# A hybrid attention layer on one core: a stated order on ScalarE and VectorE for the first rotated tiles

## The chip, the cores and the metric

The kernel runs as one program on 1 core of a Trainium2 chip. The metric is the device time of one execution in microseconds (us). Before the change three runs took 1109.55, 1108.88 and 1105.74 us; their median is 1108.88. A core has TensorE (PE: matmuls, and PEld: loading their weights), VectorE (DVE), ScalarE (ACT), GpSimd (POOL) and SyncE (SP, which here only issues transfers). Each works through its own queue of instructions in order and waits for the others through semaphores.

## What is computed

One encoder layer over 1024 tokens of width 1024, in float32. The input is normed and projected once; the columns of the projection feed two attentions, whose normed outputs go through one output projection, and then a gated MLP with a short convolution follows. What the change touches is the start of the first attention (8 query heads in 2 groups, each with one key and one value head, a window of 128 tokens to each side, and rotary embedding on a quarter of the dimensions):

```python
hn = rmsnorm(h, norm_mix[l])
proj = jnp.einsum('bsd,de->bse', hn, w_in[l])
qa, ka, va, qb, kb, vb = jnp.split(proj, splits, axis=-1)
qa = partial_rope(qa.reshape(B, S, A_HEADS, HEAD_DIM), cos, sin)
ka = partial_rope(ka.reshape(B, S, A_KV_HEADS, HEAD_DIM), cos, sin)
va = va.reshape(B, S, A_KV_HEADS, HEAD_DIM)
o_a = window_gqa_sink(qa, ka, va, sink[l])
o_b = neighbourhood_attention(...)
...
def partial_rope(t, cos, sin):
    half = ROT_DIM // 2
    x1 = t[..., :half]
    x2 = t[..., half:ROT_DIM]
    return jnp.concatenate([x1 * cos - x2 * sin, x2 * cos + x1 * sin, t[..., ROT_DIM:]], axis=-1)
```

## The kernel before

**Tiles.** Everything is kept with features in partitions and tokens along the free axis. The input projection is made in 18 tiles `m` of 128 features. For the first head group, m = 0 holds the key head (partitions 0 to 63) and the value head (64 to 127), and m = 1 and 2 hold two query heads each; m = 3, 4, 5 are the same for the second group. From m = 6 on come the tiles of the second attention.

**Precision.** A float32 factor is split into a high part, which ScalarE makes with a copy, and a low part, which VectorE makes by subtracting the high part from the source. `halve_w` does so for weights (L126 high, L127 low), in halves of four blocks of 128 rows: `load_w` and `Project.load` take blocks 0 to 3, `Project.load_rest` takes 4 to 7. A product is then three matmuls a block (L134 to L136: high by high, high by low, low by high); a tile of 128 features by 1024 tokens takes two halves `h` of 512 tokens, each of 8 blocks, so 24 matmuls. The high and the low weights have three buffers each, the raw weights two.

**From a projected tile to the scores.** A half tile stands in a PSUM bank until `evacuate` (L189, VectorE) multiplies it by the norm's reciprocal and writes it to the tile `t`. Projections use two banks by turns ("pj"); the first three tiles use others as well. Then, for m = 0 to 5, `post` runs:

- `split_v` (m = 0 and 3 only): TensorE transposes the value half (L269), ScalarE copies it (L273), VectorE makes the low part (L274).
- `rotate`: transfers fold the rows to be rotated out into a compact tile `f` (L205: one on ScalarE's queue, one on SyncE's); VectorE multiplies, multiplies and adds (L207 twice, L208, L209); SyncE sends the rows back into `t` (L211 twice). There are three sets of scratch for it: two in the tile `f`, one in `turns`.
- the stacks: the tile, split in high and low parts, laid out in 128 partitions as the scores need it. For the first group no transfers are used: `split_first_k` makes `ka` and `kb` with two ScalarE copies (L235, L238) and two VectorE subtractions (L236, L237), `split_first` makes two `q` tiles with two ScalarE copies (L228) and two VectorE operations (L229).

A score tile (L309) is two matmuls of such stacks into one of two "s" banks. `softmax` frees the bank: VectorE adds the mask and takes the row extremum (L331), ScalarE takes the exponential with a sum (L335), VectorE inverts the sums of a pair of tiles (L337), GpSimd scales (L339). TensorE then transposes the tiles (L371), and so on.

**Order.** TensorE's order is that of the source (`manual_schedule`). On the other engines a scheduler picks by priority among what is ready by its own estimate; `tc.high_priority` lifts a block. The projections are a generator, `rest()`, whose steps (one block of three matmuls each) are woven between the attention's steps by `fill`. The first three tiles are projected before it starts, m = 2 with weights of its own (`raw3`, `whi3`, `wlo3`). `FILL0 = 22` steps run before the first scores: the 16 of m = 3, and 6 of m = 4. The stacks of m = 2 are made by `settle` within `rest()`, those of m = 0 and 1 ahead of it. m = 4's second weights are traced at step 11 (`REST`) of m = 3. The tile `t` of m = 0 to 3 is cut from one pool of three buffers (`tmp`), so m = 3's `t` needs a buffer that an earlier tile has left.

Of the kernel before, what the change touches and what calls it, by code (L numbers as in the profile page):

```python
# [53 lines left out]
def hybrid_layer(tc, xT, w_in, w_out, w_gate, w_up, w_down, small, sink, rpb, consts, rope, out):  # L54
    nc = tc.nc
    with ExitStack() as ctx:
# [13 lines left out]
        def big(name, tag, dt=F32):  # L70
            return lpool.tile([128, S], dt, name=name, tag=tag, bufs=slots[tag])
# [42 lines left out]
            nc.tensor.matmul(warm_ps[:, 0:128], ones, ones, start=True, stop=True)  # L114


        def fetch_w(src):

            raw = wpool.tile([128, 4, 128], F32, name="raw", tag="raw", bufs=2)
            nc.sync.dma_start(raw, src)  # L120
            return raw

        def halve_w(raw):

            hi, lo = (wpool.tile([128, 4, 128], F32R, name=n, tag=n) for n in ("whi", "wlo"))
            nc.scalar.activation(hi, raw, AF.Copy)  # L126
            nc.vector.tensor_tensor(lo, raw, f32(hi[:, :, :]), op=ALU.subtract)  # L127
            return [(hi[:, j, :], lo[:, j, :]) for j in range(4)]

        def load_w(src):  # L130
# [55 lines left out]

        def evacuate(t, ps, h, grid):
            if not grid:
                nc.vector.tensor_tensor(t[:, tsl(h)], ps, rstd1[:, tsl(h)], op=ALU.mult)  # L189
            else:  # L190
                v = lambda ap: ap.rearrange("p (r b c) -> p r b c", b=NB, c=8)
                o = t[:, :].rearrange("p (b r c) -> p r b c", r=ROWS, c=8)[:, 8 * h:8 * h + 8]
                nc.vector.tensor_tensor(o, v(ps[:, :]), v(rstd1[:, tsl(h)]), op=ALU.mult)

        folded = []

        def rotate(t, n):

            m = slice(0, n)
            f, u = folded[0]  # L200
            folded.append(folded.pop(0))
            rows = lambda s: t[4 * s:n:8].rearrange("a (c w) -> a c w", w=128)
            fold = lambda s: f[m, s]
            for s in range(2):
                (nc.scalar, nc.sync)[s].dma_start(fold(s), rows(s))  # L205
            for s in range(2):
                nc.vector.tensor_tensor(u[m, s], f[m, 1 - s], rs[m, s], op=ALU.mult)  # L207
            nc.vector.tensor_tensor(f[m], f[m], rc[m], op=ALU.mult)  # L208
            nc.vector.tensor_tensor(f[m], f[m], u[m], op=ALU.add)  # L209
            for s in range(2):  # L210
                nc.sync.dma_start(rows(s), fold(s))  # L211

        def split_pair(t):

# [9 lines left out]
        def split_first(t):  # L224

            a, b = big("q", "op", F32R), big("q", "op", F32R)
            for x, hi, lo in ((a, slice(0, 64), slice(64, 128)), (b, slice(64, 128), slice(0, 64))):
                nc.scalar.activation(x[hi], t[hi], AF.Copy, scale=-HD ** -0.5)  # L228
                nc.vector.scalar_tensor_tensor(x[lo], t[hi], -HD ** -0.5, f32(x[hi, :]), op0=ALU.mult, op1=ALU.subtract)  # L229
            return [a, b]  # L230

        def split_first_k(t):
            a, b = big("ka", "op", F32R), big("kb", "op", F32R)
            up, down = slice(0, 64), slice(64, 128)
            nc.scalar.activation(a[up], t[up], AF.Copy)  # L235
            nc.vector.tensor_tensor(b[up], t[up], f32(a[up, :]), op=ALU.subtract)  # L236
            nc.vector.tensor_tensor(a[down], t[up], f32(a[up, :]), op=ALU.subtract)  # L237
            nc.scalar.activation(b[down], t[up], AF.Copy)  # L238
            return a, b
# [13 lines left out]
        def split_k(t, e):  # L253

            a, b = big("ka", "op", F32R), big("kb", "op", F32R)
            o = 64 - e
            nc.scalar.activation(a[e:e + 64], t[e:e + 64], AF.Copy)
            nc.sync.dma_start(f32(b[o:o + 64, :]), f32(a[e:e + 64, :]))
            nc.vector.tensor_tensor(b[e:e + 64], t[e:e + 64], f32(a[e:e + 64, :]), op=ALU.subtract)
            nc.sync.dma_start(f32(a[o:o + 64, :]), f32(b[e:e + 64, :]))  # L260
            return a, b

        def split_v(t, halves):

            v = [big("v", "op", F32R) for _ in halves]
            for g in range(2):
                ps = bank("vt", "pt")
                for c in range(4):
                    nc.tensor.transpose(ps[:, c * 128:(c + 1) * 128], t[:, (4 * g + c) * 128:(4 * g + c + 1) * 128], ident)  # L269
                for i, e in enumerate(halves):  # L270
                    src = ps[:, :].rearrange("p (c w) -> p c w", w=128)[:, :, e * 64:e * 64 + 64]
                    dst = v[i][:, :].rearrange("p (c w) -> p c w", w=128)[:, 4 * g:4 * g + 4]
                    nc.scalar.activation(dst[:, :, 0:64], src, AF.Copy)  # L273
                    nc.vector.tensor_tensor(dst[:, :, 64:128], src, f32(dst[:, :, 0:64]), op=ALU.subtract)  # L274
            return [x[:, :].rearrange("p (c w) -> p c w", w=128) for x in v]

        qa, ka, va, qb, kb, vb = {}, {}, {}, {}, {}, {}
        mix = [None] * 8

        def post(m, t):  # L280

            if m < 6:
                g, i = divmod(m, 3)
                if i == 0:
                    va[g] = split_v(t, (1,))[0]
                    rotate(t, 64)
                    ka[g] = split_k(t, 0) if g else split_first_k(t)
                else:
                    rotate(t, 128)
                    qa[g, i - 1] = split_pair(t) if g else split_first(t)  # L290
            else:
                hp, i = divmod(m - 6, 3)
                if i == 0:
                    vb[2 * hp], vb[2 * hp + 1] = split_v(t, (0, 1))
                else:
                    h = 2 * hp + i - 1
                    qb[h], kb[h] = split_qk(t)
# [183 lines left out]
        class Project:  # L481
# [10 lines left out]
            def run(self):  # L492
                self.t = tmp("t")
                if self.m < 17:
                    for h in range(2):
                        ps = bank("pj", "pj")
                        yield from product(ps, self.w, xg, h)
                        with tc.high_priority(offset=500):
                            evacuate(self.t, ps, h, self.grid)
                else:  # L500

                    ps = [bank("pj", "pj") for _ in range(2)]
                    for k in range(KT):
                        for h in range(2):
                            block(ps[h], self.w[k], xg[k], h, k == 0, k == KT - 1)
                            yield
                        if k % 2:
                            mg[k // 2] = split(mix[k // 2], "mg", "xg")
                    for h in range(2):
                        evacuate(self.t, ps[h], h, self.grid)  # L510
# [84 lines left out]
        nc.scalar.activation(hi, raw, AF.Copy)  # L595
        nc.vector.tensor_tensor(lo, raw, f32(hi[:, :]), op=ALU.subtract)
        third.w = [(hi[:, 128 * k:128 * k + 128], lo[:, 128 * k:128 * k + 128]) for k in range(KT)]
        third.t = tmp("t")
        ps3 = [bank("s", "s") for _ in range(2)]
        for _ in product(ps3[0], third.w, xg, 0):  # L600
            pass
# [14 lines left out]
        for _ in rest3:  # L616
            pass
        for p in first:
            with tc.high_priority(offset=400):
                p.post()  # L620
        for h in range(2):
            evacuate(third.t, ps3[h], h, False)

        live = {"op": 0}
        needs = lambda m: 2 if m < 6 and m % 3 else 2 if m >= 6 and m % 3 == 0 else 3
        waiting = [third]

        def settle(age):

            while waiting and (len(waiting) > 1 or age >= (LATE if waiting[0].m == 3 else LAG)):  # L630
                m = waiting[0].m
                if live["op"] + needs(m) > slots["op"]:
                    break
                live["op"] += needs(m)
                with tc.high_priority(offset=400 if m == 2 else 0):
                    waiting.pop(0).post()

        aux = {}
# [1 line left out]
        def rest():  # L640
            for i, job in enumerate(jobs[1:]):
                if i + 2 < len(jobs):
                    jobs[i + 2].load()
                for n, _ in enumerate(job.run()):
                    yield True
                    if n == REST and i + 2 < len(jobs):
                        jobs[i + 2].load_rest()
                    settle(n)
                    if (i, n) in aux:
                        aux[i, n]()  # L650
                if isinstance(job, Project):
                    waiting.append(job)
                while len(waiting) > 2:
                    settle(0)
                    if len(waiting) > 2:
                        yield False
# [18 lines left out]
        for i in range(4):  # L675
            aux[13, 3 * i + 3] = normed_a(i)
        filler = rest()
        live["op"] = sum(needs(m) for m in (0, 1))

        def fill(n):  # L680
            while n > 0 and next(filler, False):
# [736 lines left out]
```

## Time and profile before

| | |
|---|---|
| runs, us | 1109.55, 1108.88, 1105.74 |
| median, us | 1108.88 |
| profiled execution: its own time, us | 1108.75 |
| its span, from first to last instruction, us | 1106.7 |
| mean granted clock of TensorE | 0.995 |
| TensorE busy | 98% of the span |
| VectorE / ScalarE / GpSimd busy | 77% / 50% / 10% |

The durations below come from the one profiled execution. Its own time is 2.05 us longer than its span. In a row of the timeline stand the start in us from the span's beginning, the duration, the engine, the line of the kernel, the operation, the tile written and those read, the sizes, how many such rows were merged, and in brackets how long the engine had been idle and which instruction it had waited for. "ACTq" and "SPq" are the engines' queues that issue transfers. Matmuls are pipelined, so the start of the next one, not the shown duration, is their pace.

### The profile page before, as it was taken

What the parts mean: (1) busy time and instruction counts of PE and PEld (TensorE: products, weight loads), DVE (VectorE), ACT (ScalarE), POOL (GpSimd) and SP (SyncE); (2) the same over time, 40 slices, a digit from 0 to 9 for tenths busy, and PEclk for the clock granted to TensorE, in tenths of its full rate; (3) what the DMA queues carried; (4) which work ended last, traced back from release to release, by engine and by line L of the source; (5) the groups of instructions that cost most, each with busy time, mean ns of one, the idle gap of its engine ahead of it and who ended that gap; (6) DMA issues with size and microseconds to landing.
All of it is one profiled execution on the core that took longest, in us unless ns stands there. A gap on an engine that the chain in (4) does not pass through costs nothing.

```text
span 1106.7 us, 15054 instructions
## 1 busy us (share of the span) xinstructions
PE 1082.4 (98%) x5190; PEld 903.6 (82%) x5190; DVE 857.7 (77%) x1565; ACT 551.6 (50%) x1041; POOL 108.7 (10%) x188
## 2 busy tenths in 40 slices
PE   9989999999999999999999999999999999999997
PEld 7868888888888888787788888888888878888887
DVE  7478888667688687899988877877887868886844
ACT  7257766656666544454444334342434644544531
POOL 2213333222232100000000000000000000000001
PEclk9999999999999999999999999999999999999999
DMA  7213122232225237304433222323322889874734
GB/s 270 71 51 79 49 66 65 70 86 67 77 64 156 68 106 264 106 11 145 167 121 127 105 105 96 113 97 116 104 86 105 272 287 300 267 224 159 270 95 153
DMA packets 68364, 144.94 MB, mean 131 GB/s; under 512 B 8128, under 2 KB 18880, under 8 KB 68288
## 3 DMA queue, kind: packets, MB, share of 16 engines
q1 hardware_dynamic: 57632, 118.16, 34.4%
q10 hardware_dynamic: 10656, 25.82, 6.2%
q8 instruction: 40, 0.66, 0.2%
q14 instruction: 36, 0.29, 0.1%
HBM read 103.58 MB, written 28.57 MB: 119 GB/s over the span
## 4 chain that ended last, share of the span: by engine, by line
PE 84%; DVE 9%; DMA 3%; ACT 2%; issue 2%; ACTq 0%; POOL 0%; SPq 0%; DVEq 0%; POOLq 0%
PE dn L826 6%; PE pj L134 6%; PE dn L828 6%; PE dn L827 6%; PE pj L135 6%; PE pj L136 6%; PE z L828 5%; PE z L826 5%; PE z L827 5%; PE s L309 3%; PE x L826 3%; PE x L827 3%; PE x L828 3%; PE y L828 3%; PE y L827 3%; PE y L826 3%
## 5 line engine op out<-in xcount | busy, mean ns | idle before, releaser
L826 PE MATMUL dn<-xd,whi 128*128 128x512 f32 (+1 forms) x330 | 124.9, 378 | 2.8 <-ACT c L1254 2.8
L828 PE MATMUL dn<-xd,wlo 128*128 128x512 f32 (+1 forms) x330 | 124.2, 376 | 0.0
L827 PE MATMUL dn<-xd,whi 128*128 128x512 f32 (+1 forms) x330 | 124.2, 376 | 0.0
L815 ACT ACTIVATE whi<-ws 128x512 fp32r<-128x512 f32 (+1 forms) x100 | 60.1, 623 | 124.1 <-DVE ws L932 82.5
L134 PE MATMUL pj<-xgh,whi 128*128 128x512 f32 x248 | 104.6, 422 | 3.1 <-DVE t L189 3.1
L828 PE MATMUL z<-hg,wlo 128*128 128x512 f32 x264 | 103.1, 390 | 0.6 <-DVE wlo L816 0.6
L826 PE MATMUL z<-hg,whi 128*128 128x512 f32 x264 | 103.0, 390 | 0.2 <-DVE gs L982 0.2
L827 PE MATMUL z<-hg,whi 128*128 128x512 f32 x264 | 102.7, 389 | 0.0
L335 ACT ACTIVATE p<-p,nm 128x385 f32<-128x385 f32 (+3 forms) x128 | 74.9, 586 | 46.9 <-DVE nm L331 46.2
L136 PE MATMUL pj<-xgh,wlo 128*128 128x512 f32 x248 | 98.3, 396 | 0.0
L135 PE MATMUL pj<-xgl,whi 128*128 128x512 f32 x248 | 98.0, 395 | 0.0
L339 POOL TENSOR_SCALAR p<-p,sm 128x384 f32<-128x384 f32 (+1 forms) x128 | 73.4, 586 | 222.0 <-DVE sm L337 207.4
L816 DVE TENSOR_TENSOR wlo<-raw,whi 128x512 fp32r<-128x512 f32 (+1 forms) x102 | 66.3, 670 | 21.8 <-ACT whi L815 20.9
L345 DVE TENSOR_TENSOR pl<-pt,ph 128x384 fp32r<-128x384 f32 (+2 forms) x108 | 63.0, 588 | 24.8 <-ACT ph L344 23.7
L815 ACT ACTIVATE whi<-raw 128x512 fp32r<-128x512 f32 (+1 forms) x102 | 60.4, 611 | 41.7 <-DMA raw<-in_w_down_dram 19.0
L816 DVE TENSOR_TENSOR wlo<-ws,whi 128x512 fp32r<-128x512 f32 (+1 forms) x100 | 66.7, 681 | 18.4 <-ACT whi L815 18.3
L1137 ACT ACTIVATE xd<-xd 128x512 fp32r<-128x512 f32 x77 | 47.1, 627 | 59.4 <-DMA xd<-x 59.1
L1245 POOL TENSOR_TENSOR h<-h,wide 128x256 f32<-128x256 f32 (+1 forms) x6 | 5.4, 925 | 719.8 <-ACT wide L1241 719.8
L826 PEld LDWEIGHTS dn<-xd,whi 128*128 128x128 f32 x330 | 62.5, 189 | 14.2 <-ACT c L1254 3.2
L827 PEld LDWEIGHTS dn<-xd,whi 128*128 128x128 f32 x330 | 62.6, 190 | 11.2
L828 PEld LDWEIGHTS dn<-xd,wlo 128*128 128x128 f32 x330 | 62.4, 189 | 11.4
L344 ACT ACTIVATE ph<-pt 128x384 fp32r<-128x384 f32 (+2 forms) x108 | 55.0, 513 | 32.7 <-PE pt L444 25.2
(209 smaller groups left out, 2687.8 us busy)
## 6 DMA issues: line engine op xcount, KB each, us to landing
xd<-x SPq DMA_DIRECT2D x77, 256.0 KB, 5.0
raw<-in_w_down_dram SPq DMA_DIRECT2D x72, 256.0 KB, 4.1
raw<-in_w_gate_dram SPq DMA_DIRECT2D x22, 512.0 KB, 3.5
raw<-in_w_up_dram SPq DMA_DIRECT2D x22, 512.0 KB, 3.6
x<-c ACTq DMA_DIRECT2D x22, 512.0 KB, 2.6
raw<-in_w_in_dram SPq DMA_DIRECT2D x32, 256.0 KB, 2.8
raw<-in_w_down_dram SPq DMA_DIRECT2D x36, 192.0 KB, 3.9
x<-t ACTq DMA_DIRECT2D x11, 512.0 KB, 2.6
```

The source lines that it names most:

```text
L134: nc.tensor.matmul(ps, w[0], x[0][:, tsl(h)], start=first, stop=False)
L135: nc.tensor.matmul(ps, w[0], x[1][:, tsl(h)], start=False, stop=False)
L136: nc.tensor.matmul(ps, w[1], x[0][:, tsl(h)], start=False, stop=last)
L335: nc.scalar.activation(p[:, j, 0:e], p[:, j, 0:e], AF.Exp, bias=nm, scale=-1.0, accum_out=sm[:, j:j + 1])
L339: nc.gpsimd.tensor_scalar(p[:, i, 0:m], p[:, i, 0:m], sm[:, i:i + 1], 1.0, op0=ALU.mult, op1=ALU.mult)
L344: nc.scalar.activation(ph[:, 0:n], ps[:, 0:n], AF.Copy)
L345: nc.vector.tensor_tensor(pl[:, 0:n], ps[:, 0:n], f32(ph[:, 0:n]), op=ALU.subtract)
L815: nc.scalar.activation(hi, src, AF.Copy)
L816: nc.vector.tensor_tensor(lo, src, f32(hi[:, :, :]), op=ALU.subtract)
L826: nc.tensor.matmul(ps, w[0], x[0], start=first and i == 0, stop=False, skip_group_check=True)
L827: nc.tensor.matmul(ps, w[0], x[1], start=False, stop=False, skip_group_check=True)
L828: nc.tensor.matmul(ps, w[1], x[0], start=False, stop=last and i == len(ws) - 1, skip_group_check=True)
```

## The change

Each marked instruction is kept in a dictionary `mark`, and `behind(names)` puts the instructions traced in a block, on the engine of the marked one, behind it in that engine's queue. No wait is added by this; it fixes places in the queues.

```diff
+        mark = {}
+        def behind(*names):
+            stack = ExitStack()
+            for n in names:
+                stack.enter_context(tc.issue_after(mark[n].ins))
+            return stack
...
-            nc.scalar.activation(hi, raw, AF.Copy)
-            nc.vector.tensor_tensor(lo, raw, f32(hi[:, :, :]), op=ALU.subtract)
+            mark["weights"] = nc.scalar.activation(hi, raw, AF.Copy)
+            mark["weights low"] = nc.vector.tensor_tensor(lo, raw, f32(hi[:, :, :]), op=ALU.subtract)
...
-        def rotate(t, n):
+        def rotate(t, n, order=()):
...
-            nc.vector.tensor_tensor(f[m], f[m], u[m], op=ALU.add)
-            for s in range(2):
-                nc.sync.dma_start(rows(s), fold(s))
+            mark["turned"] = nc.vector.tensor_tensor(f[m], f[m], u[m], op=ALU.add)
+            with behind(*order):
+                back = [nc.sync.dma_start(rows(s), fold(s)) for s in range(2)]
+            mark["back"] = back[1]
...
+        def turn(m, t):
+            g, i = divmod(m, 3)
+            if i == 0:
+                va[g] = split_v(t, (1,))[0]
+            rotate(t, 64 if i == 0 else 128, ["back"] * (m in (1, 2)))
+        def stacks(m, t):
+            g, i = divmod(m, 3)
+            if i == 0:
+                ka[g] = split_k(t, 0) if g else split_first_k(t)
+            else:
+                qa[g, i - 1] = split_pair(t) if g else split_first(t)
...
-                        with tc.high_priority(offset=500):
+                        with tc.high_priority(offset=500), behind(*["low"] * (self.m == 3 and h == 1)):
                             evacuate(self.t, ps, h, self.grid)
...
-        third.t = tmp("t")
+        third.t = big("t", "mix")
...
         for p in first:
-            with tc.high_priority(offset=400):
-                p.post()
+            with tc.high_priority(offset=400), behind(*["turned"] * p.m):
+                turn(p.m, p.t)
         for h in range(2):
             evacuate(third.t, ps3[h], h, False)
+        with tc.high_priority(offset=400):
+            with behind("turned"):
+                turn(third.m, third.t)
+            with behind("value"):
+                nc.scalar.activation(warm, eps, AF.Exp)
...
-        waiting = [third]
+        waiting = []
+        def make_stacks(job):
+            with tc.high_priority(offset=400):
+                stacks(job.m, job.t)
+            done.add(job.m)
...
-                with tc.high_priority(offset=400 if m == 2 else 0):
+                with behind(*["stack", "low"] * (m == 3)):
                     waiting.pop(0).post()
...
-                    jobs[i + 2].load()
+                    with behind(*["stack"] * (i == 1)):
+                        jobs[i + 2].load()
                 for n, _ in enumerate(job.run()):
                     yield True
+                    if i == 0:
+                        if n == 8:
+                            with behind("copied"):
+                                for p in first:
+                                    make_stacks(p)
+                        continue
...
+                if i == 0:
+                    with behind("stack", "copied"):
+                        jobs[2].load_rest()
+                    with behind("weights", "weights low"):
+                        make_stacks(third)
...
-        live["op"] = sum(needs(m) for m in (0, 1))
+        live["op"] = sum(needs(m) for m in range(3))
```

`mark` is also set for the last ScalarE copy and VectorE operation of the first group's q stacks ("stack", "low"), the value copies ("value") and the plain evictions ("copied").

What the queues look like as built, around the change:

| | before | after |
|---|---|---|
| ScalarE, from the second value copy | weights (m=4, second half), ka, kb, q, q, q, q, weights (m=5), load of exponential's table, exponentials | load of exponential's table, one exponential of 128x1, ka, kb, q, q, weights (m=4, second half), q, q, weights (m=5), exponentials |
| VectorE, rotations | the operations of m=0 and 1 mixed, then m=2 | m=0, m=1, m=2 one after the other |
| VectorE, after them | low weights (m=4), kb, ka, q, both evictions of m=3, q, q, q, low weights (m=5), rotation of m=3, six row extrema, reciprocals | first eviction of m=3, kb, ka, q, q, second eviction of m=3, low weights (m=4), q, q, four row extrema, reciprocal, low weights (m=5), fifth extremum, reciprocal, sixth extremum, eviction of m=4, rotation of m=3 with a reciprocal between |
| SyncE | rows back of m=1, m=0, m=2; load of m=5's second weights, fetch of m=3's rows, next loads | rows back of m=0, m=1, m=2; fetch of m=3's rows, load of m=5's second weights, next loads |

TensorE's and GpSimd's lists are the same before and after. Further on, one low-weights operation on VectorE changes places with the value operation behind it, and one load of weights on SyncE goes behind two stack transfers of the second attention.

More of the change, by code (lines that the diff above doesn't have):

```diff
@@ L188, in evacuate @@
             if not grid:
-                nc.vector.tensor_tensor(t[:, tsl(h)], ps, rstd1[:, tsl(h)], op=ALU.mult)
+                mark["copied"] = nc.vector.tensor_tensor(t[:, tsl(h)], ps, rstd1[:, tsl(h)], op=ALU.mult)
             else:
@@ L227, in split_first @@
             for x, hi, lo in ((a, slice(0, 64), slice(64, 128)), (b, slice(64, 128), slice(0, 64))):
-                nc.scalar.activation(x[hi], t[hi], AF.Copy, scale=-HD ** -0.5)
-                nc.vector.scalar_tensor_tensor(x[lo], t[hi], -HD ** -0.5, f32(x[hi, :]), op0=ALU.mult, op1=ALU.subtract)
+                mark["stack"] = nc.scalar.activation(x[hi], t[hi], AF.Copy, scale=-HD ** -0.5)
+                mark["low"] = nc.vector.scalar_tensor_tensor(x[lo], t[hi], -HD ** -0.5, f32(x[hi, :]), op0=ALU.mult, op1=ALU.subtract)
             return [a, b]
@@ L272, in split_v @@
                     dst = v[i][:, :].rearrange("p (c w) -> p c w", w=128)[:, 4 * g:4 * g + 4]
-                    nc.scalar.activation(dst[:, :, 0:64], src, AF.Copy)
+                    mark["value"] = nc.scalar.activation(dst[:, :, 0:64], src, AF.Copy)
                     nc.vector.tensor_tensor(dst[:, :, 64:128], src, f32(dst[:, :, 0:64]), op=ALU.subtract)
@@ L278, in hybrid_layer @@
         mix = [None] * 8
+        def turn(m, t):
[9 more added lines that the diff above has]
+                qa[g, i - 1] = split_pair(t) if g else split_first(t)
         def post(m, t):
             if m < 6:
[L283 to L290, printed above, removed]
+                turn(m, t)
+                stacks(m, t)
             else:
```

## The prediction

> **What bounds the kernel now.** I read the page first, for which engine sets the end.
>
> ```profile
> span 1106.7 us, 15054 instructions
> PE 1082.4 (98%) x5190; PEld 903.6 (82%) x5190; DVE 857.7 (77%) x1565; ACT 551.6 (50%) x1041; POOL 108.7 (10%) x188
> PE 84%; DVE 9%; DMA 3%; ACT 2%; issue 2%; ACTq 0%; POOL 0%; SPq 0%; DVEq 0%; POOLq 0%
> ```
>
> TensorE is busy nearly throughout and holds 84% of the chain that ended last. So only two things can shorten this kernel: time in which TensorE stands still, and time in which it runs slowly. The next view is what TensorE waits for (total us, times, longest):
>
> ```profile
> PE pj L134 <- DVE t L189: 3.1, 1, 3.1
> PE dn L826 <- ACT c L1254: 2.8, 1, 2.8
> ```
>
> The longest wait is one matmul of a projection, waiting for an eviction of `t` on VectorE; the second, near 910 us, is far from this change. Next the busy times by stretch (columns: PE, PEld, DVE, ACT, POOL, then granted clock, DMA share, GB/s):
>
> ```profile
> 57.20:60.40 3.20, 0.08 (x2) 0.07 (x1) 3.17 (x4) 3.13 (x4) 0.00 (x0) 1.00 0.18 63
> 60.30:64.10 3.80, 3.77 (x10) 2.96 (x11) 3.71 (x4) 1.67 (x2) 0.00 (x0) 0.55 0.07 17
> 64.10:66.20 2.10, 2.10 (x11) 1.73 (x10) 2.03 (x5) 0.00 (x0) 0.00 (x0) 1.00 0.00 0
> 910.70:913.60 2.90, 2.67 (x6) 2.15 (x7) 2.90 (x6) 2.11 (x5) 0.00 (x0) 0.50 0.93 267
> ```
>
> TensorE stands still from 57.2 to 60.3, and when it restarts its granted clock is 0.55 until 64.1, then 1.00. The wait near 910 us is followed by a clock of 0.50 too. The same stretch on TensorE, in order of time:
>
> ```profile
> 51.61 0.39 PE L134 MATMUL pj<-xgh,whi 128*128 128x512 f32 x1
> 56.82 0.39 PE L136 MATMUL pj<-xgh,wlo 128*128 128x512 f32 x1
> 60.33 0.53 PE L134 MATMUL pj<-xgh,whi 128*128 128x512 f32 x1 [3.12 <-DVE t L189]
> 60.66 0.62 PE L135 MATMUL pj<-xgl,whi 128*128 128x512 f32 x1
> 64.08 0.40 PE L134 MATMUL pj<-xgh,whi 128*128 128x512 f32 x1
> 66.14 0.28 PE L309 MATMUL s<-ka,q 128*128 128x256 f32 x1
> ```
>
> 51.61 begins the second half (24 matmuls) of projection m=3; 56.82 is its last. So a matmul takes (56.82 − 51.61) / 23 = 0.227 us. 60.33 begins m=4; 18 of its matmuls run before the first scores at 66.14. Why the eviction was late is read on ScalarE and VectorE:
>
> ```profile
> 46.77 0.38 ACT L273 ACTIVATE v<-vt 128x256 fp32r<-128x256 f32 x1 [0.49 <-DVE v L274]
> 54.35 0.63 ACT L126 ACTIVATE whi<-raw 128x512 fp32r<-128x512 f32 x1 [7.19 <-PE pj L135]
> 54.89 1.05 ACT L235 ACTIVATE ka<-t 64x1024 fp32r<-64x1024 f32 x1
> 57.04 4.29 ACT L228 ACTIVATE q<-t 64x1024 fp32r<-64x1024 f32 x4
> ...
> 50.13 0.42 DVE L209 TENSOR_TENSOR turns<-turns 128x256 f32<-128x256 f32 x1
> 55.02 0.69 DVE L127 TENSOR_TENSOR wlo<-raw,whi 128x512 fp32r<-128x512 f32 x1 [4.46 <-ACT whi L126]
> 55.97 1.22 DVE L236 TENSOR_TENSOR kb<-t,ka 64x1024 fp32r<-64x1024 f32 x1 [0.26 <-ACT ka L235]
> 57.20 1.22 DVE L237 TENSOR_TENSOR ka<-t,ka 64x1024 fp32r<-64x1024 f32 x1
> 58.34 1.21 DVE L229 SCALAR_TENSOR_TENSOR q<-t,q 64x1024 fp32r<-64x1024 f32 x1
> 59.58 1.29 DVE L189 TENSOR_TENSOR t<-pj,rstd 128x512 f32<-128x512 f32 x2
> 60.90 3.72 DVE L229 SCALAR_TENSOR_TENSOR q<-t,q 64x1024 fp32r<-64x1024 f32 x3
> 65.27 0.48 DVE L207 TENSOR_TENSOR f<-f,turns 64x128 f32<-64x128 f32 x2
> 66.58 0.48 DVE L331 CUSTOM_DVE_ANT_0 p<-s,cst,nsink 128x256 f32<-128x256 f32 x1
> ```
>
> ScalarE's queue is in order, and at its head from 47.15 stands the copy of m=4's second weights, which needs a buffer that TensorE frees only at 54.3: 7.19 us idle. The stack copies queue behind it. VectorE idles 4.46 us behind the same copy, and both evictions of m=3 (L189 x2) stand behind the first stacks. The first half's bank was full at about 51.8 and is emptied at 59.58.
>
> **The change part by part.** *Removed: the wait and the slow clock after it.* In the built order VectorE evicts the first half of m=3 right after the third tile's rotation, and that tile no longer takes a buffer from the three that m=3's `t` is cut from. So this eviction depends on its bank (51.38 + 0.39 = 51.8) and the rotation (50.13 + 0.42 = 50.6) alone: 51.8 to 52.5, long before m=4 starts. TensorE then goes on at 56.82 + 0.23 = 57.05, and after 18 x 0.227 = 4.10 us reaches the scores at 61.15 instead of 66.14: **4.99 us earlier**. Of it 60.33 − 57.05 = 3.28 is the wait, and 66.14 − 60.33 − 4.10 = 1.71 the slow clock (from 60.66 to 64.08 eight matmuls take 0.43 each).
>
> *Moved: the stacks and the weights, which must now meet 61.15.* The rotated rows must come back first:
>
> ```profile
> 48.87 2.60 SPq L211 DMA_DIRECT2D t<-f  x4
> 51.56 1.20 SPq L211 DMA_DIRECT2D t<-turns  x2
> DMA to landing us min/median/max: 2.0/2.0/2.0
> ```
>
> Before, the second tile's two transfers left first and the K tile's third and fourth. Now the K tile's go first: 48.87 and 49.52 at the latest (the rotation ahead of them is now shorter), so rows at 49.52 + 2.0 = 51.5. ScalarE: `ka` to 52.55, `kb` 53.6, two q 55.75 (4.29 / 4 = 1.07 each), weights 56.4 (their buffer is free at 54.3), two q 58.5. VectorE, by start-to-start times from the rows above: `kb` from 52.55, 1.23; `ka` 1.14; two q 2 x 1.24; second eviction (bank full at 57.2) 1.32 / 2 = 0.66, to 58.1; low weights 0.69, to 58.8; two q 2.48, to 61.28. TensorE needs the low weights at the 15th matmul of m=4, 57.05 + 14 x 0.227 = 60.2: met by 1.4 us. The first maximum (L331) followed the first scores by 66.58 − 66.14 = 0.44, so it could start at 61.59: met by 0.3. That 0.3 is the whole cover of this chain.
>
> The landing of the K tile's rows is the unknown. From below it is 51.5. From above: before, ScalarE took these rows at 54.89 without waiting, and they now leave two transfers (1.30 us) earlier: 53.6. Then VectorE's chain starts at 54.65 and ends at 63.4, 1.8 us after 61.59, which TensorE waits out at the third score. I take 51.5, as the landing time is 2.0 in all its rows; the range keeps 1.8.
>
> *Added: the early load of exponential's table, and one tiny exponential.*
>
> ```profile
> 67.15 1.28 ACT L335 ACT_TABLE_LOAD   x1 [5.16 <-DVE nm L331]
> 73.28 0.63 ACT L126 ACTIVATE whi<-raw 128x512 fp32r<-128x512 f32 x1 [1.55 <-issue]
> 73.94 0.69 DVE L127 TENSOR_TENSOR wlo<-raw,whi 128x512 fp32r<-128x512 f32 x1 [2.02 <-ACT whi L126]
> 75.67 0.86 DVE L274 TENSOR_TENSOR v<-vt,v 128x256 fp32r<-128x256 f32 x2 [1.03 <-ACT v L273]
> raw<-in_w_in_dram SPq DMA_DIRECT2D x32, 256.0 KB, 2.8
> ```
>
> 1.28 us, and at most 0.4 for the exponential (its nearest row, a 128x256 copy at 46.77, takes 0.38), lie in ScalarE's idle time from 47.15 to 51.5: nothing. Without that cover they would delay `ka`, so all that follows, by 1.7. The load that leaves 67.15 frees ScalarE, not TensorE: nothing.
>
> *Work pushed behind the scores.* m=3's four rotation operations (65.27 to 66.65, 1.38 us) and one low-weights copy (0.69) now come after, 2.1 us of VectorE. There it idles 2.02 and 1.03 us (73.94 and 75.67): nothing, at most 2.1 without that cover. Two reciprocals that wait for exponentials now stand ahead of the fifth and sixth maxima; by the chain above the fifth comes at about 64.0, against 68.93 − 4.99 = 63.9 before, so nothing.
>
> *SyncE.* The load of m=5's second weights moves behind the fetch of m=3's rows (after the eviction at 58.1), and waits for the low weights at 58.8: issued about 59, landed by 62 with 2.8. Its reader is the copy at 73.28, which comes 5 us earlier, at 68.3: 6 us of slack. Later one load slips behind two stack transfers:
>
> ```profile
> 211.97 0.47 SPq L248 DMA_DIRECT2D q<-kb  x1
> 220.63 0.63 ACT L126 ACTIVATE whi<-raw 128x512 fp32r<-128x512 f32 x1 [0.31 <-PE pj L135]
> ```
>
> It would be issued at about 212.5 and land at 215.3, for a reader at 220.63: nothing.
>
> **Sum.** The profiled execution took 1108.75 us, 2.05 outside its span, and is 0.13 under the median, 1108.88. 1108.75 − 4.99 = **1103.8**. TensorE's own order is the same from end to end, so what it gains here it keeps unless a later wait grows.
>
> **The rivals.** *The slow clock stays, 1105.5.* If the clock of 0.55 came from something other than the wait, only 3.28 goes. For it: a program could fall into a slow phase here by its own age. Against: both long waits of the profile (3.1 and 2.8) are followed by a half clock at once, and no row shows it elsewhere.
> [...]
> *Rows land late, 1105.6:* the 1.8 above. For it: the landing isn't seen in these rows. Against: 2.0 in all others.
> *Given back, 1108.7.* Units 0 to 10 may be paced by VectorE, which then makes TensorE wait later for what it skipped here.
>
> ```profile
> 80.00:100.00 20.00, 20.00 (x107) 17.05 (x106) 18.23 (x50) 15.32 (x37) 6.92 (x18) 1.00 0.40 98
> ```
>
> For it: VectorE is 91% busy there. Against: TensorE is 100% busy there, and VectorE's own stack work also moves up, by the 4.46 us in which it idled.
> *Slower, 1112.7.* m=3's second eviction, the low weights and the last stacks now stand on VectorE behind stacks that wait for the returned rows. Each us by which these land after 51.8 costs one. At 51.8 + 4.99 = 56.8 the old time is reached; if the wait also halves the clock (1.71), at 55.1. Landing at 59.0, they cost 7.2 + 1.71 − 4.99 = 3.9: 1112.7. For it: the queue is in order, with a cover of only 0.3. Against: those rows were there by 54.89 when they left later.
>
> **How the numbers follow.** Forecast 0.70, slow clock 0.08, late rows 0.07, given back 0.10, slower 0.05. The forecast's own range is 1102.2 (the half clock after 910 us, 2.9 us at 0.50, doesn't come and saves 1.5) to 1105.3 (half of both unknowns). Taking in the two rivals near 1105.5 with the spread of the runs (1105.74 to 1109.55), the range is 1101.9 to 1106.6. About 0.3%, 3.3 us, is what can be told from no change: below 1105.6 is faster. Nearly all of the forecast and half of the two middle rivals lie there, 0.77; same 0.18; slower 0.05.
>
> **What would show it.** Right: no wait of `pj` L134 for `t`; clock 1.00 from 50 to 70 us; an eviction at about 51.8; first scores near 61.2 and the table load near 47.2; TensorE 5 us ahead at 80 and still at 400 us. Wrong: a new wait at the scores or the third score above 0.5 us (late rows); a slow clock near 60 us without a wait; the lead at 400 us smaller than at 80 (given back).

## The result and the profile after

| | before | after |
|---|---|---|
| median of nine runs each, us | 1108.88 | 1101.24 |
| lowest to highest, us | 1104.56 to 1112.12 | 1100.17 to 1104.37 |
| after over before, with its 95% interval | | 0.9945 [0.9929, 0.9962] |
| profiled execution, its own time, us | 1108.75 | 1103.74 |
| its span, us | 1106.7 | 1101.9 |
| mean granted clock | 0.995 | 0.996 |

The change makes the kernel faster, by 0.55%, or 6.1 us of 1108.88 (4.2 to 7.9 by the interval). The ratio on record is not that of the two medians: these lie 7.6 us apart here, and 5.5 when both kernels ran once more (`a_again` below). The forecast's own ratio, 1103.8 / 1108.75 = 0.9955, lies inside the interval. Its time is 2.6 us above this median of 1101.24, which is also 0.7 under the predicted range; by the ratio the changed kernel stands at 1108.88 x 0.9945 = 1102.8, inside it. The profiled execution, 1103.74, is the slowest but one of the nine.

From the page of the kernel after come the shares of the chain that ended last, and from its waits the longest one of TensorE:

```profile
PE 86%; DVE 7%; DMA 3%; ACT 2%; issue 2%; POOL 0%; SPq 0%; DVEq 0%; ACTq 0%; POOLq 0%
PE dn L866 <- ACT c L1294: 2.3, 1, 2.3
```

The wait of `pj` for `t` is gone; what was second before (2.8, near 910 us) is now first. VectorE's share of the chain falls from 9% to 7%. Next, what each engine does around the change, in order of time: TensorE, ScalarE and VectorE, and below them the busy times from 50 to 70 us.

```profile
45.60 0.48 PE L144 MATMUL pj<-xgh,whi 128*128 128x512 f32 x1
56.59 0.39 PE L144 MATMUL pj<-xgh,whi 128*128 128x512 f32 x1
60.67 0.28 PE L327 MATMUL s<-ka,q 128*128 128x256 f32 x1
61.74 0.36 PE L327 MATMUL s<-ka,q 128*128 128x256 f32 x1 [0.44 <-DVE nm L349]
...
46.72 1.28 ACT L645 ACT_TABLE_LOAD   x1
50.49 1.06 ACT L246 ACTIVATE ka<-t 64x1024 fp32r<-64x1024 f32 x1 [2.27 <-DMA t<-f]
...
51.35 0.69 DVE L199 TENSOR_TENSOR t<-pj,rstd 128x512 f32<-128x512 f32 x1 [1.10 <-PE pj L146]
51.96 1.21 DVE L247 TENSOR_TENSOR kb<-t,ka 64x1024 fp32r<-64x1024 f32 x1
57.42 0.68 DVE L137 TENSOR_TENSOR wlo<-raw,whi 128x512 fp32r<-128x512 f32 x1
58.14 2.47 DVE L240 SCALAR_TENSOR_TENSOR q<-t,q 64x1024 fp32r<-64x1024 f32 x2
61.11 0.48 DVE L349 CUSTOM_DVE_ANT_0 p<-s,cst,nsink 128x256 f32<-128x256 f32 x1 [0.50 <-PE s L327]
63.73 0.61 DVE L349 CUSTOM_DVE_ANT_0 p<-s,cst,nsink 128x384 f32<-128x384 f32 x1
...
50.00:70.00 20.00, 19.38 (x93) 15.89 (x91) 16.22 (x32) 11.88 (x22) 3.52 (x6) 1.00 0.14 43
```

45.60 is the first matmul of m = 3. In the profile of before it started at 46.05:

```profile
46.05 0.48 PE L134 MATMUL pj<-xgh,whi 128*128 128x512 f32 x1
```

So this execution came 0.45 us earlier to the place of the change, by its head (what runs before that matmul) and not by the change; 0.45 is added below to its times before they are compared with the prediction. m = 4 begins at 56.59 behind m = 3 with no wait, the clock is 1.00, and the first scores start at 60.67 + 0.45 = 61.12 against 66.14.

How far this lead carries is read on TensorE alone, from the first matmul of m = 3 to the start of the last scores of the first two attentions. Heads and tails, which differ between executions by up to 1.4 us, are then left out. The rows by tile show the last start ("first and last start"), before, then after:

```profile
L309 PE MATMUL s<-ka,q x128: 274/337/442, 66.1 to 374.6; 128*128 128x384 f32 x96, 128*128 128x256 f32 x32
```
```profile
L327 PE MATMUL s<-ka,q x128: 274/337/445, 60.7 to 369.6; 128*128 128x384 f32 x96, 128*128 128x256 f32 x32
```

That is 374.6 − 46.05 = 328.6 us before and 369.6 − 45.60 = 324.0 after: 4.6 of the 5.0 are still there at 370 us. The same measure of every profiled kernel (rows of the same two kinds; the experiments follow):

| kernel | first of m = 3 | last scores | between, us |
|---|---|---|---|
| before | 46.05 | 374.6 | 328.6 |
| before, once more (`b_again`) | 46.42 | 375.2 | 328.8 |
| before, with the third tile's buffer alone (`b_mix`) | 45.57 | 374.4 | 328.8 |
| after | 45.60 | 369.6 | 324.0 |
| after, once more (`a_again`) | 45.76 | 370.3 | 324.5 |
| after, later copies ordered too (`a_left`) | 46.05 | 370.2 | 324.2 |
| after, without the early table load (`a_noexp`) | 46.29 | 370.6 | 324.3 |
| after, first eviction behind the stacks (`a_short`) | 46.23 | 371.0 | 324.8 |
| after, weights ahead of the stacks (`a_wfirst`) | 45.76 | 373.0 | 327.2 |
| after, rotations in no stated order (`a_mixrot`) | 46.02 | 373.4 | 327.4 |

Where the 0.4 went is seen at 352 us: TensorE now waits there for a transfer of SyncE, `kb<-ka`, of a later stack. Below are before (the issue on SyncE, the matmul that reads it, and the busy times from 335 to 355 us), then after, then `a_again`:

```profile
351.67 0.46 SPq L250 DMA_DIRECT2D kb<-ka  x1
357.09 0.27 PE L309 MATMUL s<-kb,q 128*128 128x256 f32 x1
335.00:355.00 20.00, 19.20 (x104) 16.06 (x103) 17.87 (x41) 13.76 (x32) 5.19 (x8) 1.00 0.55 144
```
```profile
345.52 0.46 SPq L261 DMA_DIRECT2D kb<-ka  x1
351.55 0.28 PE L327 MATMUL s<-ka,q 128*128 128x256 f32 x1
351.90 0.39 PE L327 MATMUL s<-kb,q 128*128 128x256 f32 x1
```
```profile
352.62 0.38 PE L327 MATMUL s<-kb,q 128*128 128x256 f32 x1 [0.70 <-DMA kb<-ka]
335.00:355.00 20.00, 18.50 (x97) 15.22 (x96) 16.24 (x36) 12.23 (x27) 3.34 (x6) 1.00 0.70 189
```

Before, the matmul comes 0.11 us after its neighbour and finds its data there, 5.4 us after the issue; after, it comes 0.35 behind its neighbour, so 0.24 late, 6.4 us after the issue; in `a_again` it waits 0.70, at a DMA share of 0.70 against 0.55 before. `a_left` and `a_noexp` wait there too (0.38 and 0.47). Of the kernels that come later to this place `a_wfirst` is not late, but `a_mixrot` is by 0.21, and the kernel before once more (`b_again`) by 0.10. So the last tenths of a lead are taken back here, and some of it is not the change's own. What slows this transfer among those under way stays open.

Behind 400 us the executions differ in waits that also differ between two executions of one kernel. Before waited 1.1 us for `h` near 440 us (`b_again` 0.2), after did not; after waited 1.0 for `gs` (`a_again` 0.3), before 0.2. By the last matmul after is 6.2 us ahead (1093.58 against 1099.76), and its last transfers then take 1.4 us longer (8.3 against 6.9 to the end of the span). The 5.0 between the two profiled times is therefore 5.0 at the scores, less 0.4, and a balance of such differences; that it equals the forecast's 4.99 is luck.

### The profile page after: what moved, and what is told of

Its sections match the earlier page's. It is cut to its first block, busy times and chain, and to the rows that moved or that the text cites. A ratio compares the mean times of both kernels' runs of the same rounds, so it can differ in the third digit from the quotient of the medians.

```text
span 1101.9 us, 15051 instructions
## 1 busy us (share of the span) xinstructions
PE 1079.2 (98%) x5190; PEld 901.0 (82%) x5190; DVE 858.5 (78%) x1565; ACT 552.9 (50%) x1042; POOL 109.2 (10%) x188
## 4 chain that ended last, share of the span: by engine, by line
PE 86%; DVE 7%; DMA 3%; ACT 2%; issue 2%; POOL 0%; SPq 0%; DVEq 0%; ACTq 0%; POOLq 0%
PE pj L144 7%; PE pj L145 7%; PE pj L146 7%; PE dn L866 6%; PE dn L867 6%; PE dn L868 6%; PE z L868 5%; PE z L866 5%; PE z L867 5%; PE x L866 3%; PE s L327 3%; PE x L867 3%; PE x L868 3%; PE y L868 3%; PE y L867 3%; PE y L866 3%
```

## The experiments

In the expectations, T is the account of the prediction with what the result added to it; R with a number is a rival, as each text states it. The kernel before ran again beside all of them: 1107.41 us (24 runs) on the chip of `b_again`, `a_again`, `b_mix` and `a_left`, and 1108.25 us (33 runs) on that of the other four. Ratios are against the before of the same chip.

### Both kernels once more: `b_again`, `a_again`

No edit.

> The kernel before, unchanged, profiled once more. Theory T (the lead of the change is TensorE's wait for the evictions of m=3 and the half clock that the wait brings; what lies beyond these 5.0 us differs from run to run): the wait before the first matmul of m=4 is again 3.1 us within 0.2, a half clock follows within 1 us of its end, and the wait of VectorE for a transfer of gate weights near 440 us (2.7 us in the first profile) differs from it by more than 0.5. Time 1108.9, ratio to itself 1.000 within 0.2%. Rival R1 (the clock falls by the program's age): the half clock comes at another distance from the restart, or not at all, though the wait is there. Rival R2 (the change shortens a later stage for good): the wait near 440 us is there again within 0.3 us.

> The kernel after, unchanged, profiled once more. T: no wait above 0.5 us on TensorE between 46 and 80 us, clock 1.00 from 50 to 80 us, first scores 5.0 us earlier against the start of m=3 than in the kernel before (15.1 us after the first matmul of m=3, against 20.1). Time 1101 to 1104, ratio 0.9935 to 0.9955. R1: a half clock shows between 46 and 80 us without a wait. R2: the lead of TensorE grows by over 0.5 us between 300 and 470 us again in this pair of profiles.

Measured: `b_again` 1109.76 us, ratio 1.0015 [0.9998, 1.0032]; `a_again` 1101.91 us (1101.16 to 1103.92), ratio 0.9946 [0.9923, 0.9968]. The first row of the waits of `b_again` is the same as before, 3.1 us of `pj` for `t`, and the clock is again halved right after that wait; TensorE's wait near 440 us is 0.2 here instead of 1.1:

```profile
PE x L826 <- DVE h L845: 0.2, 1, 0.2
60.96:64.37 3.41, 3.41 (x9) 2.63 (x9) 3.32 (x4) 1.38 (x2) 0.00 (x0) 0.50 0.08 19
```

The result repeats, and the wait and the half clock belong to the kernel before. VectorE's wait for gate weights near 440 us was 2.27 us, against 2.65 before: a difference of 0.4, less than the expected 0.5. That the change shortens this later stage for good (R2) is not seen even so: from 300 to 470 us TensorE's lead, taken at the same matmuls, grew by 1.4 us in the first pair of profiles and fell by 1.0 in this one, and `a_noexp`, a changed kernel, waits 1.1 us for `h` again.

### The third tile's own buffer alone: `b_mix`

```diff
-        third.t = tmp("t")
+        third.t = big("t", "mix")
```

On the kernel before. This lets the evictions of m = 3 go ahead of the stacks on VectorE, where the scheduler then puts them; ScalarE keeps its old order, with the weights ahead of the stacks.

> One part alone: the kernel before, with the third tile's t taken from the other pool. Both evictions of m=3 then stand ahead of the first stacks on VectorE (the second one behind the low weights), ScalarE's order is as before. T: the wait of 3.1 us at m=4's first matmul goes, but the stacks still stand behind the weights that TensorE frees at 54.3: stacks from 57.9, 2 x 1.23 + 4 x 1.22 us long, so the last is ready at 65.3 where the scores could begin at 61.2; TensorE waits some 3 to 4 us at the first to third scores instead, with a half clock behind it. Time 1107 to 1108.5, a gain of 0.5 to 2 us: the order of the stacks against the weights is the other half of the change. Rival R3 (the eviction is all there is to it, the stacks have slack): 1104, ratio 0.9955.

Measured: 1107.76 us, ratio 0.9999 [0.9981, 1.0018]. VectorE, TensorE and one stretch of its profile:

```profile
51.32 0.69 DVE L189 TENSOR_TENSOR t<-pj,rstd 128x512 f32<-128x512 f32 x1 [1.19 <-PE pj L136]
59.73 4.96 DVE L229 SCALAR_TENSOR_TENSOR q<-t,q 64x1024 fp32r<-64x1024 f32 x4
64.73 0.48 DVE L331 CUSTOM_DVE_ANT_0 p<-s,cst,nsink 128x256 f32<-128x256 f32 x1
...
65.36 0.36 PE L309 MATMUL s<-ka,q 128*128 128x256 f32 x1 [2.61 <-DVE nm L331]
...
66.58:69.99 3.41, 3.41 (x10) 2.93 (x11) 2.29 (x9) 3.28 (x12) 0.93 (x2) 0.50 0.26 77
```

The eviction goes at 51.32, m = 4 does not wait, and the scores come at 61.0. But the stacks still stand behind the copy of m = 4's second weights, VectorE makes them until 64.7, and the third score waits 2.61 us for the first maximum. With two waits of 0.20 and 0.75 for `q` ahead of it that is 3.6 us at the scores, as expected. The half clock follows that wait. The expected gain of 0.5 to 2 us is not seen (328.8 against 328.6 and 328.8): the stall was moved, with its half clock, from the projection to the scores. The buffer alone brings nothing.

### The weights ahead of the stacks: `a_wfirst`

```diff
                         if n == 8:
-                            with behind("copied"):
+                            jobs[2].load_rest()
+                            with behind("copied", "weights", "weights low"):
                                 for p in first:
                                     make_stacks(p)
...
                 if i == 0:
-                    with behind("stack", "copied"):
-                        jobs[2].load_rest()
-                    with behind("weights", "weights low"):
-                        make_stacks(third)
+                    make_stacks(third)
```

On the kernel after: the other half of the change is undone, and the buffer and the rest of the order stay.

> The kernel after, but m=4's second weights go back ahead of the stacks on ScalarE and VectorE; the evictions and the rotations stay as in the change. T (two halves: evictions early, stacks ahead of those weights): ScalarE waits for TensorE until 53.9, stacks from there; chain on VectorE: kb at 55.6, ka 56.8, q 58.0, q 59.2, eviction 60.4, q, q to 63.5, so the first row extremum at 63.6 against 61.1, 2.5 us late. No wait at m=4's first matmul; a wait of about 2.5 us more than after at the third score; time 1104.4, up to 1106 in profiles in which a half clock follows. R3 (the stacks have slack): 1101.9, as after.

Measured: 1106.91 us (1102.98 to 1109.85), ratio 0.9986 [0.9973, 0.9999]. ScalarE, TensorE and one stretch:

```profile
54.06 0.63 ACT L136 ACTIVATE whi<-raw 128x512 fp32r<-128x512 f32 x1 [5.67 <-issue]
54.59 1.05 ACT L246 ACTIVATE ka<-t 64x1024 fp32r<-64x1024 f32 x1
...
64.41 0.45 PE L327 MATMUL s<-ka,q 128*128 128x256 f32 x1 [2.94 <-DVE nm L349]
64.52:67.93 3.41, 3.33 (x10) 2.87 (x11) 2.95 (x13) 2.53 (x9) 1.65 (x3) 0.50 0.00 1
```

ScalarE stands 5.67 us before the weights copy, `ka` starts 4.1 us later than in the kernel after, and the third score waits 2.94 us instead of 0.44. The 2.5 us are as expected, and so is a half clock behind them, for which the expectation allowed up to 1106; the median is 0.9 above that. The trace is of one of the two fastest of the twelve runs (1102.98), so it does not show what the slower ones lost. Together with `b_mix`: the buffer, even with the rotations in order, brings 0.1% as long as the weights stand ahead of the stacks. The stated order without the tile's own buffer was not tried, so that the buffer is needed is not shown. The next run speaks against it being worth much, by argument alone: there the eviction goes behind the last reader of the K tile's `t`, when the pool of three would have a buffer to give, and most of the gain stays (ratio 0.9965).

### The first eviction behind the first stacks: `a_short`

```diff
-                        with tc.high_priority(offset=500), behind(*["low"] * (self.m == 3 and h == 1)):
+                        with tc.high_priority(offset=500), behind(*["low"] * (self.m == 3)):
...
-                        if n == 8:
+                        if n == 7:
```

> The kernel after, with the first eviction of m=3 put behind the stacks of m=0 and 1 instead of ahead of them, so that its bank comes free at about 57.0 where TensorE would take it at 56.6. T: a wait of 0.3 to 1.0 us at m=4's first matmul, and no half clock behind it (a wait costs its own length as long as it leaves most of a stretch of 3.4 us busy); then the rotation of m=3 ahead of the first extremum, up to 0.8 more at the third score. Time 1102.2 to 1103.6. Rival (any wait here halves the clock): 1.7 more, 1104 to 1105.3, with a clock of 0.5 in the stretch after it.

Measured: 1103.1 us (1101.2 to 1107.61), ratio 0.9965 [0.995, 0.9979]. VectorE and TensorE:

```profile
57.07 1.29 DVE L199 TENSOR_TENSOR t<-pj,rstd 128x512 f32<-128x512 f32 x2
57.82 0.50 PE L144 MATMUL pj<-xgh,whi 128*128 128x512 f32 x1 [0.43 <-DVE t L199]
```

m = 4 waits 0.43 us by its row and the clock stays at 1.00. Without the head TensorE is 0.7 us behind the kernel after from the scores to 340 us; to the last scores it is 0.3 to 0.8 (324.8 against 324.5 and 324.0). The third score waits 0.44 us, no more than in the kernel after, so the further 0.8 at the third score did not come. The same eviction, late by little, cost its lateness; before, late by 3 us, it also cost the half clock.

### The rotations in no stated order: `a_mixrot`

```diff
-            rotate(t, 64 if i == 0 else 128, ["back"] * (m in (1, 2)))
+            rotate(t, 64 if i == 0 else 128)
...
-            with tc.high_priority(offset=400), behind(*["turned"] * p.m):
+            with tc.high_priority(offset=400):
```

> The kernel after without the stated order of the rotations and of the transfers that bring their rows back: the K tile's rows then leave as the last of six transfers, issued by about 52.8 and landed by 54.1, against 50.5 in the kernel after. By the price of the prediction (each us past the cover costs one; the cover was 0.5 in the profile of after): stacks on VectorE start at 55.2 instead of 52.0, 3.2 less 0.5 = 2.7 us later scores; 1104.6, up to 1106.3 if a half clock follows. Rival (the stacks' order has more slack than the chain shows): below 1103.

Measured: 1104.97 us (1102.07 to 1108.86), ratio 0.9974 [0.9957, 0.9991]. ScalarE and TensorE:

```profile
54.98 1.06 ACT L246 ACTIVATE ka<-t 64x1024 fp32r<-64x1024 f32 x1 [6.33 <-DMA t<-f]
62.29 0.78 PE L146 MATMUL pj<-xgh,wlo 128*128 128x512 f32 x1 [1.55 <-DVE wlo L137]
```

The K tile's rows now leave last and are there at 54.98 instead of 50.49. The low weights of m = 4, behind the stacks on VectorE, come 1.55 us late, a half clock follows (62.34 to 65.75), and TensorE is 2.9 to 3.4 us behind at the last scores. The size is near the expected 2.7, but the wait is at the low weights; the third score, where the expectation had it, waits 0.25 us. This is the "slower" rival of the prediction at a smaller size, the chain of late rows, late stacks and late weights.

### Without the early table load: `a_noexp`

```diff
-            with behind("value"):
-                nc.scalar.activation(warm, eps, AF.Exp)
```

> The kernel after without the early exponential (its table is loaded right before the first softmax tile again). T: nothing waits for it: the load lies in idle time of ScalarE in both places; TensorE's starts agree with the kernel after within 0.2 us from the first scores to 300 us; ratio to before as after, 0.9945 within 0.002. Rival R4 (the early table carries part of the gain, up to its 1.28 us): 0.9957, and TensorE later by 1 us at the first transposes.

Measured: 1102.4 us (1100.11 to 1107.59), ratio 0.9958 [0.9943, 0.9974], which cannot be told from 0.9946 or 0.9945 with the load. The trace decides: the load now stands ahead of the first exponential,

```profile
62.37 1.28 ACT L353 ACT_TABLE_LOAD   x1 [3.53 <-DVE nm L349]
```

and TensorE needs 324.3 us to the last scores, between the 324.0 and 324.5 with the load. This trace is of the slowest of its eleven runs (1107.59), but what that one lost, it lost behind 340 us: up to there TensorE's starts agree with those of the kernel after within 0.03 us, once the heads (0.69) are taken out. Loading the table early is worth nothing that can be measured here.

### One more stated order, near 905 us: `a_left`

The wait that is now the longest has the same cause as the one removed. ScalarE's rows in the kernel after, then TensorE's:

```profile
903.38 0.63 ACT L1177 ACTIVATE xd<-xd 128x512 fp32r<-128x512 f32 x1 [2.27 <-DMA xd<-x]
903.91 0.58 ACT L1294 ACTIVATE c<-dn 128x512 f32<-128x512 f32 x1
...
904.55 0.50 PE L866 MATMUL dn<-xd,whi 128*128 128x512 f32 x1 [2.33 <-ACT c L1294]
```

The copy `c` frees TensorE's bank, and stands in ScalarE's queue behind a split of `xd` that waits 2.27 us for its load. The edit puts the splits behind the copies:

```diff
-                nc.scalar.activation(c_at(j), ps, AF.Copy)
+                mark["left"] = nc.scalar.activation(c_at(j), ps, AF.Copy)
...
-                    x_split(p + 1, q - 1)
+                    with behind(*["left"] * ("left" in mark)):
+                        x_split(p + 1, q - 1)
```

> The kernel after, with the same means used on the next wait: in the last stage the splits of loaded blocks (xd) are put behind the copies that empty the first four banks (c), which stood behind splits that wait for their loads (TensorE waits 2.3 us there and runs at half clock for 3.4 us). If T holds for waits of this kind, that wait and the half clock after 900 us go: 2.3 + 1.5 = 3.8 us at most, 1098 to 1100, provided that the splits don't become late; if they do, a wait for xd of the next product takes its place and the time is 1101 to 1104, as after.

Measured: 1099.04 us (1098.06 to 1100.73), ratio 0.9914 [0.9892, 0.9936], the fastest kernel of the study: 8.4 us under the before beside it (1107.41) and 2.9 under `a_again`. Its ScalarE, and its busy times there:

```profile
903.32 0.58 ACT L1294 ACTIVATE c<-dn 128x512 f32<-128x512 f32 x1
906.33 0.63 ACT L1177 ACTIVATE xd<-xd 128x512 fp32r<-128x512 f32 x1 [2.43 <-DMA xd<-x]
895.00:915.00 20.00, 20.00 (x89) 16.55 (x89) 12.95 (x22) 11.02 (x21) 0.00 (x0) 1.00 0.93 309
```

ScalarE still waits 2.43 us for a load, but with the copy done; TensorE is busy for the whole 20 us, at a clock of 1.00.

## Why the prediction was right

- *The wait and the slow clock, 4.99.* Measured at the first scores 66.14 − 61.12 = 5.02. The first eviction went at 51.35 + 0.45 = 51.8, as forecast. The term held to 0.03 us.
- *The cover of 0.3 on VectorE's chain.* (Unrounded, its terms end at 61.23 instead of 61.28.) The first maximum waited 0.50 us for its score, so VectorE was done 0.50 early. `ka` started at 50.49 + 0.45 = 50.9, where 51.5 was taken: the lower bound of the landing was right, and even 0.6 too cautious. VectorE gained only about 0.15 from that, as its `kb` stood behind the first eviction until 51.96 + 0.45 = 52.4 (forecast 52.55). The price of late rows, one us for each, was too high: in `a_mixrot` they are there at about 55.0, which by the prediction costs 3.2 past 51.8 and 1.71 for the half clock, 4.9; measured were 2.9 to 3.4. TensorE waited 1.55, and the trace fits VectorE catching up while the clock was halved.
- *The low weights of m = 4, met by 1.4.* They were done at about 58.1 for a matmul at 56.59 + 14 x 0.227 = 59.77: met by 1.7, so this term held.
- *The table load at nothing.* It ran at 46.72 + 0.45 = 47.2, and ScalarE still idled 2.27 us behind it. `a_noexp` shows nothing gained or lost.
- *The work pushed behind the scores, nothing.* The fifth maximum came at 63.73 + 0.45 = 64.2 (forecast 64.0), and TensorE was 5.5 us ahead at the first row of `o` (77.5 against 83.0), 5.05 without the head.
- *"What it gains here it keeps unless a later wait grows."* One grew: the lead falls by 0.4 to 0.8 us at 352 us, to a transfer that the prediction did not look at. At 402 us the lead is 5.1, 4.65 without the head. This is the rival "given back", at about a tenth of its size and from DMA, not from VectorE.
- *The median.* The ratio's 6.1 is 1.1 more than the forecast, and 4.99 is within its interval. A little of it may be the clock: its mean over the runs on one chip is 0.9952 before and 0.9971 in `a_again`, by an estimate 0.0019 x 1105 = 2.1 us, of which 1.71 is the half clock that the forecast already counts. Whether the rest is chance stays open.

Of the rivals, "the slow clock stays" fell (1.00 from 50 to 70 us, and a half clock near 60 us only in the kernels that wait there for 1.5 us or more), and "rows land late" fell.

## What to carry to other kernels

A long wait of the busiest engine for a queue that is itself waiting can be a question of order: look on the engine named for the instruction at the head of its queue, and for what stands behind it that could already run. Here one such place was worth 5 us (with one more buffer) and another 3, and no instruction was made faster. Freeing a buffer without the order only moved the stall to the next reader, so follow the chain to that reader before counting the gain.

## What the runs showed of the hardware

The half clock comes in pieces of one length. The windows below are cut where the granted clock changes, or would change by the same steps: two each of before, after, `a_again`, `a_wfirst`, `a_mixrot` and `a_noexp` (first column after the length: TensorE's busy time, then its weight loads; the granted clock is third from the end).

```profile
57.24:60.66 3.42, 0.33 (x1) 0.30 (x2) 3.39 (x4) 3.35 (x4) 0.00 (x0) 1.00 0.16 56
60.66:64.07 3.41, 3.41 (x9) 2.64 (x8) 3.32 (x4) 1.31 (x2) 0.00 (x0) 0.50 0.08 19
```
```profile
901.68:905.10 3.42, 1.08 (x5) 0.59 (x4) 1.29 (x3) 1.72 (x4) 0.00 (x0) 1.00 0.90 287
905.10:908.51 3.41, 3.41 (x9) 2.63 (x8) 3.41 (x7) 3.31 (x7) 0.00 (x0) 0.50 0.81 249
```
```profile
904.33:907.75 3.42, 2.07 (x9) 1.73 (x10) 2.58 (x5) 3.05 (x6) 0.00 (x0) 1.00 0.81 275
907.75:911.16 3.41, 3.41 (x17) 2.82 (x16) 3.12 (x6) 2.30 (x5) 0.00 (x0) 1.00 0.75 220
```
```profile
904.18:907.59 3.41, 1.77 (x8) 1.16 (x7) 1.28 (x3) 1.95 (x4) 0.00 (x0) 1.00 1.00 314
907.59:911.00 3.41, 3.41 (x16) 2.81 (x15) 3.41 (x8) 3.15 (x7) 0.00 (x0) 1.00 0.74 225
```
```profile
58.93:62.34 3.41, 1.76 (x8) 0.82 (x6) 3.32 (x5) 3.34 (x5) 0.00 (x0) 1.00 0.00 0
62.34:65.75 3.41, 3.16 (x9) 2.51 (x10) 3.28 (x6) 0.63 (x2) 0.00 (x0) 0.50 0.33 96
```
```profile
906.69:910.10 3.41, 2.53 (x6) 2.05 (x7) 3.04 (x6) 3.22 (x7) 0.00 (x0) 0.50 0.96 306
910.10:913.51 3.41, 3.41 (x9) 2.63 (x9) 3.41 (x6) 2.82 (x6) 0.00 (x0) 0.50 0.84 256
```

The clock is 0.50 for 3.41 us, and then whole again: 1.00 before from 64.07 to 910.58, and in after from 908.51 to the tail. In `a_noexp` it stays at 0.50 for a second stretch. The halving near 60 us and the one near 910 us lie 910.58 − 60.66 = 849.92 us apart before, and as far in `b_again` (910.88 − 60.96). The one in the tail of before, at 1101.73, comes 191.15 behind the second, and so does the one in the tail of after, at 1096.25, behind that at 905.10. 191.15 / 56 and 849.92 / 249 are both 3.413. So within an execution the halvings fit a grid of such stretches, which does not start with the wait: the half clock begins 0.35 us ahead of the first matmul behind the wait before (910.93), and 1.22 after it in `b_mix` (66.58 − 65.36).

What goes with the halving is how busy TensorE was in the stretch before. Above, the clock was halved after 10% (before) and 32% (after), and not after 61% (`a_again`, with a part of a wait of 2.0 us in it). It was also halved after 30% before (907.16 to 910.58), 37% in `b_again` (907.47 to 910.88), 30% in `b_mix` (63.16 to 66.58), 14% in `a_wfirst` (61.11 to 64.52) and 42% in `a_noexp` (903.28 to 906.69), and not after 60% in `b_mix` (59.75 to 63.16). In none of these was TensorE idle throughout; the least work was 0.33 us. All other stretches of the two profiles of before and after, leaving out the first 40 us and the tails, were 69% or more busy, and none of them was followed by a half clock. Of the two above at 52% that in `a_mixrot` was halved and that in `a_wfirst` not, so this share alone does not decide. The first had fewer weight loads (0.82 us against 1.16), and in `a_noexp` a stretch that was 74% busy at half clock was followed by another; which activity counts stays open.

Where a wait of 2.1 to 3.1 us left a stretch 42% busy or less, the half clock followed; the one near 60 us cost 1.71 us more before, and `a_noexp` had two stretches of it. Where the grid cut a wait of 2.0 us in two (`a_again`, 80% and 61% busy), the clock stayed at 1.00; the same program can differ by this from one execution to the next, as after and `a_again` do near 905 us.
